# Splits and a product taken from GpSimd in the recurrent and gated-output stage of a hybrid S5 / RG-LRU block

## The chip, the cores and the metric

The kernel runs on one core of a Trainium2 chip. The metric is the device time of one execution in microseconds (us), the median over runs. Before the change it is 2388.78 us (three runs, 2385.07 to 2389.40).

In the text PE is the tensor engine, VectorE is DVE in the rows, ScalarE is ACT, GpSimd is POOL, and SP is the queue that issues the transfers.

## The reference

One layer of a diffusion backbone on 2048 latent tokens of 1024 channels, with 256 context tokens as prefix. What the change touches is the mixer's second half:

```
xc = centred_depthwise_conv(to_col_major(xr), conv_w, conv_b)          # 512 channels
for each direction d:
    r = sigmoid(block_diag(xc, w_rg[d], b_rg[d]));  i = sigmoid(block_diag(xc, w_ig[d], b_ig[d]))
    a = exp(-8 * r * softplus(-lam[d]))
    h[d] = linear_scan(a, sqrt(1 - a^2) * (i * xc))                    # along the sequence
y_lru = from_col_major(h[0] + h[1]) * gelu(gate)
y_s5  = y * sigmoid(y @ w_glu + b_glu)                                 # y: the S5 output, 512 channels
out   = concat(y_s5, y_lru) @ w_out
```

After it come a normed residual and a SwiGLU feed-forward network (FFN), which take the last 1460 us of the kernel.

## The kernel before

All matmuls are done in a split form: an fp32 operand is cut into a high part `hi`, a rounded copy in the matmul's type, and a low part `lo = src - hi`, and three matmuls (hi by hi, hi by lo, lo by hi) replace one. `split` writes `hi` on ScalarE (line 59) and `lo` on VectorE (line 62). `hi(..., nc.gpsimd)` (line 57) and `lo(..., nc.gpsimd)` put them on GpSimd.

The stage of interest runs from about 600 to 926 us. It has two parts that are woven into each other.

`lru` goes through four blocks m of 128 channels, each with 2308 positions (context, padding and latent). Per block: `conv(m)` loads the input, splits the gate weights (`lwh`, `lwl`), convolves on VectorE and splits the result in five chunks (`xh`, `xl`). `gates(m, d)`, for each direction, does twelve matmuls for each of the five chunks, evicts them with two sigmoids on ScalarE (`lr`, `li`, line 900) and multiplies `li` by `xc` (line 903). `decay` has Tanh, Exp and two Squares on ScalarE and two VectorE instructions per direction (lines 912 to 918). `scans` has a Sqrt on ScalarE, a product and two scans on VectorE (lines 922 to 929). Then both directions are added, multiplied by the gate branch, and stored to `YLRU`.

The filler is `glu` and `out_s5`. A `glu` step takes 256 tokens: load `gy`, split it (`gyh`, `gyl`), 48 matmuls, four VectorE bias adds from PSUM (line 1022), one Sigmoid on ScalarE (line 1023), one product, one store. There are eight. An `out_s5` tile takes 128 tokens: load `osy`, split it (`osyh`, `osyl`), and for each half of the 1024 output columns 12 matmuls and an eviction to `oso` (line 1048), then one store. There are sixteen tiles; each of `osy`, `osyh`, `osyl` and `oso` has two buffers.

How they are woven: `run` in `mix` steps `lru`, and each of its yields gives a credit of filler time, from which filler steps are traced:

```
for want in gen:
    owed += want
    while owed > 0:
        owed -= next(fill, 1e9)
```

Followed through, the credits place `glu` step 0 after `decay` of block 0, and steps 1 to 7 inside the gates of blocks 1 and 2. The splits of the `w_out` rows (`woh`) come near the end of the gates of block 2. `out_s5` tiles 0 to 2 lie inside the gates of block 3, and the first half of tile 3 after `decay` of block 3. The rest of the tiles are drained afterwards in `mix3`.

The order of the instructions on the engines is set by a planner that simulates a timeline, with one exception: `mix2` traces the loop under

```
with self.tc.manual_schedule(engines={self.nc.scalar.engine}):
    run(lru, fill)
```

so that ScalarE's instructions of this part stand in the order in which the program writes them. What is traced outside that block (the first `conv` in `mix`, the drain in `mix3`) is ordered by the planner on all engines. `glu` and `out_s5` are generators, so their steps are traced under whichever block pulls them.

After the stage, `tile_out` of the FFN reads `OSD` (the stored `out_s5` tiles) and `YLRU` and starts the second half of the output projection.

Of the kernel before, what the change touches and what calls it, by code (L numbers as in the profile page):

```python
# [12 lines left out]
AF = mybir.ActivationFunctionType  # L13
ALU = mybir.AluOpType
MUL, ADD, SUB = ALU.mult, ALU.add, ALU.subtract
# [30 lines left out]
class Hybrid:  # L46
# [783 lines left out]
    def lru(self, es, bes):  # L830


        nc, A, v = self.nc, self.A, self.nc.vector
# [26 lines left out]
        def conv(m):  # L860
            xs = p.tile([128, XC], F32, name="xs")
            nc.gpsimd.memset(xs[:, 0:2], 0.0)
            nc.gpsimd.memset(xs[:, 2 + CTX:2 + LAT], 0.0)
            nc.gpsimd.memset(xs[:, XC - 1:XC], 0.0)
            nc.sync.dma_start(xs[:, 2:2 + CTX], self.XRD[m][:, 0:CTX])
            nc.sync.dma_start(xs[:, 2 + LAT:XC - 1], self.XRD[m][:, CTX:CTX + SEQ])
            wr = p.tile([128, 4, 128], F32, name="lwr")
            wh, wl = (p.tile([128, 4, 128], F32R, name=nm, bufs=2) for nm in ("lwh", "lwl"))
            nc.gpsimd.memset(wr, 0.0)
            for i, nm in enumerate(("lru_w_rg", "lru_w_ig")):  # L870
                for h in range(2):
                    hs = slice(h * 64, (h + 1) * 64)
                    nc.sync.dma_start(wr[hs, i::2, hs], A[nm][0, :, 2 * m + h].rearrange("d a b -> a d b"))
            self.hi(wh, wr, nc.gpsimd)
            self.lo(wl, wr, wh, nc.gpsimd)
            xc = p2.tile([128, XO + 1], F32, name="xc")
            cw = lambda i: cB[:, C_CW + i * 4 + m:C_CW + i * 4 + m + 1]
            nc.gpsimd.memset(xc[:, XO:], 0.0)
            v.tensor_scalar(xc[:, :XO], xs[:, 0:XO], cw(0), cB[:, C_CB + m:C_CB + m + 1], op0=MUL, op1=ADD)
            for i in range(1, 4):  # L880
                v.scalar_tensor_tensor(xc[:, :XO], xs[:, i:i + XO], cw(i), xc[:, :XO], op0=MUL, op1=ADD)
            parts = []
            for j, (c0, n) in enumerate(CH):
                xh, xl = (p.tile([128, n], F32R, name=f"{nm}{j}") for nm in ("xh", "xl"))
                if m == 0:
                    self.split(xh, xl, xc[:, c0:c0 + n])
                else:
                    self.hi(xh, xc[:, c0:c0 + n], nc.gpsimd)
                    self.lo(xl, xc[:, c0:c0 + n], xh, nc.gpsimd)
                parts.append((xh, xl))  # L890
            return wh, wl, parts, xc

        def gates(m, d, wh, wl, parts, xc):
            ri = [(pb.tile([128, XO + 1], F32, name=nm, bufs=1) if (2 * m + d) % 3 == 2 else
                   p2.tile([128, XO + 1], F32, name=nm)) for nm in ("lr", "li")]
            for (c0, n), (xh, xl) in zip(CH, parts):
                for gt, cb in ((0, C_BRG), (1, C_BIG)):
                    pg = (psb if gt else ps).tile([128, 512], F32, name="pg")
                    self.mm3(pg[:, :n], wh[:, d * 2 + gt], wl[:, d * 2 + gt], xh, xl, True, True)
                    nc.scalar.activation(ri[gt][:, c0:c0 + n], pg[:, :n], AF.Sigmoid,  # L900
                                         bias=cB[:, cb + d * 4 + m:cb + d * 4 + m + 1])
                yield self.GATES_FILL[m]
            nc.gpsimd.tensor_tensor(ri[1], ri[1], xc, op=MUL)
            self.rit = ri

        H = (XO + 1) // 2
# [25 lines left out]
        self.wgraw = p2.tile([128, XO + 1], F32, name="xc")[:, :4 * 512].rearrange("p (k f) -> p k f", k=4)  # L932
        nc.sync.dma_start(self.wgraw, A["s5_w_glu"][0].rearrange("(k p) f -> p k f", p=128))
        x = conv(0)
        yield None
        pb = self.pool(bes, "lrub", 2, side="right")
        psb = self.pool(bes, "lrupsb", 2, side="right", space=PSUM)
        yield self.CONV_FILL
        ri = []
        for d in range(2):  # L940
            yield from gates(0, d, *x)
            ri.append(self.rit)
        for m in range(4):
            ts = [decay(m, d, ri[d][0]) for d in range(2)]
            if m == 3:

                raws = [p2.tile([128, XO + 1], F32, name="xc") for _ in range(2)]
                self.woraw = [self.raw_w_out(raws[k // 2][:, k % 2 * D:(k % 2 + 1) * D], 4 + k) for k in range(4)]
            else:
                x = conv(m + 1)  # L950
# [9 lines left out]
            if m < 3:  # L960
                yield from gates(m + 1, 0, *x)
                nxt.append(self.rit)
            gg = ri[1][1][:, :SEQ]
            nc.sync.dma_start(gg, self.GGD[m])
            y = ts[0]
# [4 lines left out]
            if m < 3:  # L970
                yield from gates(m + 1, 1, *x)
                nxt.append(self.rit)
            ri = nxt
# [20 lines left out]
    def glu(self, es):  # L994

        nc, A, v = self.nc, self.A, self.nc.vector
        p = self.pool(es, "gw", 1, side="right")
        st = self.pool(es, "gst", 2, side="right")
        ps = self.pool(es, "gps", 4, side="right", space=PSUM)
        wg = []  # L1000
        for k in range(4):
            wh, wl = p.tile([128, 512], F32R, name=f"wgh{k}"), p.tile([128, 512], F32R, name=f"wgl{k}")
            self.split(wh, wl, self.wgraw[:, k])
            wg.append((wh, wl))
        W = 256
        yield 0.1
        for n in range(8):
            y = st.tile([128, 4, W], F32, name="gy", bufs=3)
            nc.sync.dma_start(y, self.YD[:, :, n])
            yh, yl = st.tile([128, 4, W], F32R, name="gyh"), st.tile([128, 4, W], F32R, name="gyl")  # L1010
            self.hi(yh, y, nc.gpsimd)
            self.lo(yl, y, yh)
            z = st.tile([128, 4, W], F32, name="gz")
            for m in range(4):
                if m % 2 == 0:
                    pgs = ps.tile([128, 2, W], F32, name="pgl")
                pg = pgs[:, m % 2]
                ms = slice(m * 128, (m + 1) * 128)
                for k in range(4):
                    self.mm3(pg, wg[k][0][:, ms], wg[k][1][:, ms], yh[:, k], yl[:, k], k == 0, k == 3)  # L1020
                b = self.colsB[:, C_BGLU + m:C_BGLU + m + 1]
                v.tensor_scalar(z[:, m], pg, b, None, op0=ADD)
            nc.scalar.activation(z, z, AF.Sigmoid)
            v.tensor_tensor(z, z, y, op=MUL)
            nc.sync.dma_start(self.YS5[:, :, n * W:(n + 1) * W], z)
            yield 5.2

    def out_s5(self, es):

        nc, v = self.nc, self.nc.vector  # L1030
        wop = self.pool(es, "wo_a", 1, side="right")
        p = self.pool(es, "osp", 2, side="right")
        ps = self.pool(es, "osps", 4, side="right", space=PSUM)
        wo = self.split_w_out(wop, self.woraw)
        yield 10.0
        for i in range(16):
            y = p.tile([128, 4, 128], F32, name="osy")
            nc.sync.dma_start(y, self.YS5[:, :, i * 128:(i + 1) * 128])
            yh, yl = p.tile([128, 4, 128], F32R, name="osyh"), p.tile([128, 4, 128], F32R, name="osyl")
            self.hi(yh, y, nc.gpsimd)  # L1040
            self.lo(yl, y, yh)
            o = p.tile([128, D], F32, name="oso")
            for h in range(2):
                cs = slice(h * 512, (h + 1) * 512)
                po = ps.tile([128, 512], F32, name="pgl")
                for k in range(4):
                    self.mm3r(po, yh[:, k], yl[:, k], wo[k][0][:, cs], wo[k][1][:, cs], k == 0, k == 3)
                self.nc.vector.tensor_copy(o[:, cs], po)
                if h:
                    nc.sync.dma_start(self.OSD[i], o)  # L1050
                yield 2.6
# [475 lines left out]
```

## Time and profile before

| | us |
|---|---|
| median of three runs | 2388.78 |
| the profiled execution, its own time | 2388.56 |
| its span, first to last instruction | 2386.5 |
| PE busy in the span | 2125.2 |
| VectorE busy | 1750.7 |
| GpSimd busy | 1087.1 |
| ScalarE busy | 910.2 |

The profile is of one execution. Busy times do not add up to the span, since the engines work side by side. In the page's 40 slices PE shows nine tenths or more from slice 20 (1134 us) to slice 39. The stage of interest is slices 11 to 16, where PE shows 5, 4, 7, 7, 8, 8 tenths and VectorE 5, 8, 9, 8, 8, 6.

### The profile page before, as it was taken

What the parts mean: (1) busy time and instruction counts of PE and PEld (TensorE: products, weight loads), DVE (VectorE), ACT (ScalarE), POOL (GpSimd) and SP (SyncE); (2) the same over time, 40 slices, a digit from 0 to 9 for tenths busy, and PEclk for the clock granted to TensorE, in tenths of its full rate; (3) what the DMA queues carried; (4) which work ended last, traced back from release to release, by engine and by line L of the source; (5) the groups of instructions that cost most, each with busy time, mean ns of one, the idle gap of its engine ahead of it and who ended that gap; (6) DMA issues with size and microseconds to landing.
All of it is one profiled execution on the core that took longest, in us unless ns stands there. A gap on an engine that the chain in (4) does not pass through costs nothing. (4 is left out here: it accounts for less than half of the span.)

```text
span 2386.5 us, 27505 instructions
## 1 busy us (share of the span) xinstructions
PE 2125.2 (89%) x9460; PEld 1671.8 (70%) x9460; DVE 1750.7 (73%) x2293; ACT 910.2 (38%) x1434; POOL 1087.1 (46%) x665
## 2 busy tenths in 40 slices
PE   6689999896547788868999999999999999999997
PEld 2667776564436566756888888788888878888785
DVE  6975348969589886995777887987978763534688
ACT  3456521210266551554333333533333333232433
POOL 3655360325464532563333553665656530500584
PEclk8799999997678799978999999999999999999998
DMA  9465766654322447874344332554434464734583
GB/s 275 126 202 188 236 183 185 205 178 145 130 75 98 146 145 248 287 242 148 124 147 139 112 106 97 185 173 137 159 133 159 133 245 162 240 108 137 190 288 108
DMA packets 309387, 401.19 MB, mean 168 GB/s; under 512 B 59984, under 2 KB 220288, under 8 KB 307712
## 3 DMA queue, kind: packets, MB, share of 16 engines
q1 hardware_dynamic: 309120, 399.40, 51.5%
q8 instruction: 75, 1.23, 0.2%
q14 instruction: 64, 0.52, 0.1%
q0 software_dynamic: 128, 0.04, 0.0%
HBM read 268.28 MB, written 131.07 MB: 167 GB/s over the span
## 5 line engine op out<-in xcount | busy, mean ns | idle before, releaser
L70 PE MATMUL fp<-op,fws 128*128 128x512 f32 x1232 | 487.1, 396 | 9.9 <-DVE oy L1148 5.2
L71 PE MATMUL fp<-op,fws 128*128 128x512 f32 x1232 | 486.3, 395 | 4.0 <-DVE op L62 2.6
L72 PE MATMUL fp<-op,fws 128*128 128x512 f32 x1232 | 485.6, 394 | 0.0
L70 PEld LDWEIGHTS fp<-op,fws 128*128 128x128 f32 x1232 | 233.0, 189 | 64.9 <-ACT op L59 7.2
L71 PEld LDWEIGHTS fp<-op,fws 128*128 128x128 f32 x1232 | 233.3, 189 | 59.1 <-DVE op L62 4.4
L72 PEld LDWEIGHTS fp<-op,fws 128*128 128x128 f32 x1232 | 233.0, 189 | 52.1
L990 PE MATMUL po<-gw,ga 128*128 128x512 f32 x616 | 240.2, 391 | 5.2 <-ACT ga L59 2.7
L991 PE MATMUL po<-gw,ga 128*128 128x512 f32 x616 | 240.0, 391 | 0.1
L992 PE MATMUL po<-gw,ga 128*128 128x512 f32 x616 | 236.7, 390 | 2.7 <-DVE ga L62 2.7
L1284 POOL TENSOR_TENSOR fs<-fraw 128x512 f32<-128x512 f32 x44 | 64.9, 1475 | 338.3 <-DMA fraw<-in_w_ffn_in_dram 276.4
L70 PE MATMUL pu<-ht,winh 128*128 128x512 f32 (+1 forms) x448 | 176.4, 401 | 19.0 <-ACT ut L390 9.4
L71 PE MATMUL pu<-ht,winh 128*128 128x512 f32 (+1 forms) x448 | 174.7, 392 | 10.7 <-DVE ht L62 10.6
L72 PE MATMUL pu<-ht,winl 128*128 128x512 f32 (+1 forms) x448 | 172.5, 386 | 0.0
L62 DVE TENSOR_TENSOR fws<-fraw,fws 128x512 fp32r<-128x512 f32 x132 | 131.7, 999 | 48.1 <-ACT fws L59 47.2
L990 PEld LDWEIGHTS po<-gw,ga 128*128 128x128 f32 x616 | 116.2, 189 | 30.4 <-ACT ga L59 3.1
L59 ACT ACTIVATE fws<-fraw 128x512 fp32r<-128x512 f32 x132 | 82.7, 628 | 141.4 <-PE fp L72 74.5
L62 DVE TENSOR_TENSOR fws<-fs,fws 128x512 fp32r<-128x512 f32 x132 | 128.4, 973 | 9.4 <-ACT fws L59 7.3
L992 PEld LDWEIGHTS po<-gw,ga 128*128 128x128 f32 x616 | 115.5, 188 | 27.9 <-DVE ga L62 3.9
L991 PEld LDWEIGHTS po<-gw,ga 128*128 128x128 f32 x616 | 116.2, 189 | 24.8 <-DVE gw L62 0.5
L62 DVE TENSOR_TENSOR ga<-gys,ga 128x1024 fp32r<-128x1024 f32 (+2 forms) x88 | 116.5, 1328 | 12.1 <-ACT ga L59 12.0
L59 ACT ACTIVATE fws<-fs 128x512 fp32r<-128x512 f32 x132 | 82.4, 625 | 101.9 <-PE fp L72 99.0
L70 PEld LDWEIGHTS pu<-ht,winh 128*128 128x128 f32 x448 | 86.3, 195 | 45.3 <-ACT ut L390 10.3
(514 smaller groups left out, 4685.3 us busy)
## 6 DMA issues: line engine op xcount, KB each, us to landing
fraw<-in_w_ffn_in_dram SPq DMA_DIRECT2D x88, 512.0 KB, 4.4
graw<-in_w_ffn_out_dram SPq DMA_DIRECT2D x99, 256.0 KB, 3.4
gys<-S SPq DMA_DIRECT2D x44, 512.0 KB, 4.2
A<-faf SPq DMA_DIRECT2D x33, 512.0 KB, 2.6
S<-ost SPq DMA_DIRECT2D x33, 512.0 KB, 3.1
alw<-in_w_ada_dram SPq DMA_DIRECT2D x24, 512.0 KB, 4.0
ost<-A SPq DMA_DIRECT2D x22, 512.0 KB, 3.9
gys<-A SPq DMA_DIRECT2D x22, 512.0 KB, 4.8
```

Source lines behind the costliest of these rows:

```text
L59: self.nc.scalar.activation(hi, src, AF.Identity)
L62: (eng or self.nc.vector).tensor_tensor(lo, src, hi.bitcast(F32), op=SUB)
L70: mm(ps, wh, xh, start=first, stop=False)
L71: mm(ps, wh, xl, start=False, stop=False)
L72: mm(ps, wl, xh, start=False, stop=last)
L990: mm(ps, xh, wh, start=first, stop=False)
L991: mm(ps, xh, wl, start=False, stop=False)
L992: mm(ps, xl, wh, start=False, stop=last)
L1284: g.tensor_tensor(s[0], a21, a22, op=ADD)
```

## The change

Every operation that the stage gave to GpSimd, apart from memsets, is moved. The splits of the gate weights, of the convolved input of blocks 1 to 3, of the `glu` input and of the `out_s5` input become plain `split` calls: `hi` on ScalarE, `lo` on VectorE. The product of input gate and input (line 903) goes to VectorE. Of the two evictions of an `out_s5` tile the first goes to ScalarE, the second stays on VectorE. Tiles, buffers, transfers, credits and matmuls stay as they are.

```diff
-            self.hi(wh, wr, nc.gpsimd)
-            self.lo(wl, wr, wh, nc.gpsimd)
+            self.split(wh, wl, wr)
...
-                if m == 0:
-                    self.split(xh, xl, xc[:, c0:c0 + n])
-                else:
-                    self.hi(xh, xc[:, c0:c0 + n], nc.gpsimd)
-                    self.lo(xl, xc[:, c0:c0 + n], xh, nc.gpsimd)
+                self.split(xh, xl, xc[:, c0:c0 + n])
...
-            nc.gpsimd.tensor_tensor(ri[1], ri[1], xc, op=MUL)
+            v.tensor_tensor(ri[1], ri[1], xc, op=MUL)
...
-            self.hi(yh, y, nc.gpsimd)
-            self.lo(yl, y, yh)
+            self.split(yh, yl, y)          # glu, and the same in out_s5
...
-                self.nc.vector.tensor_copy(o[:, cs], po)
+                if h:
+                    v.tensor_copy(o[:, cs], po)
+                else:
+                    nc.scalar.activation(o[:, cs], po, AF.Copy)
```

## Rows read from the trace of the kernel before

**Rows 1.** Windows: engine busy us (instructions), PE's granted clock, DMA share, GB/s.
```profile
634.00:660.00 26.00, 26.00 (x164) 23.62 (x163) 19.57 (x22) 14.45 (x23) 14.97 (x14) 0.95 0.26 92
660.00:734.00 74.00, 38.98 (x224) 34.59 (x223) 62.33 (x35) 38.62 (x40) 48.33 (x30) 0.77 0.32 103
797.00:851.00 54.00, 45.53 (x190) 36.12 (x190) 48.24 (x30) 33.20 (x34) 21.09 (x11) 0.87 0.41 130
880.00:926.00 46.00, 36.75 (x156) 28.26 (x155) 34.62 (x32) 0.63 (x1) 11.08 (x9) 0.97 0.64 204
```

**Rows 2.** Waits of ScalarE, 630 to 880: total us, times, longest us.
```profile
ACT gz L1023 <- DVE gz L1022: 43.7, 4, 17.6
ACT lr L900 <- PE pg L72: 24.1, 15, 5.0
ACT lsq L917 <- DVE lt L918: 11.0, 7, 3.8
ACT lt L922 <- DVE lt L918: 5.9, 3, 2.5
```

**Rows 3.** Timeline of ScalarE: start us, us, instruction, idle before and releaser.
```profile
712.34 1.06 ACT L1023 ACTIVATE gz<-gz 128x1024 f32<-128x1024 f32 x1 [17.57 <-DVE gz L1022]
713.30 0.67 ACT L900 ACTIVATE lr<-pg,colsB 128x512 f32<-128x512 f32 x1
...
870.68 3.88 ACT L59 ACTIVATE woh<-xc 128x1024 fp32r<-128x1024 f32 x4
874.57 2.14 ACT L922 ACTIVATE lt<-lt 128x2308 f32<-128x2308 f32 x1
```

**Rows 4.** Groups of ScalarE, 600 to 925: busy us, mean ns, idle before.
```profile
L922 ACT ACTIVATE lt<-lt 128x2308 f32<-128x2308 f32 x8 | 17.1, 2134 | 5.9 <-DVE lt L918 5.9
L1023 ACT ACTIVATE gz<-gz 128x1024 f32<-128x1024 f32 x8 | 8.6, 1069 | 43.8 <-DVE gz L1022 43.7
L59 ACT ACTIVATE woh<-xc 128x1024 fp32r<-128x1024 f32 x4 | 3.9, 1042 | 0.0
L59 ACT ACTIVATE xh<-xc 128x512 fp32r<-128x512 f32 x4 | 2.2, 614 | 0.0
```

**Rows 5.** Groups of GpSimd, 600 to 925.
```profile
L903 POOL TENSOR_TENSOR li<-li,xc 128x2308 f32<-128x2308 f32 x8 | 51.4, 6427 | 14.6 <-ACT li L900 14.6
L57 POOL TENSOR_SCALAR gyh<-gy 128x1024 fp32r<-128x1024 f32 x8 | 15.4, 1929 | 6.0 <-PE pgl L72 3.5 <-DMA gy<-YD 2.5
```

**Rows 6.** Groups of VectorE, 600 to 925.
```profile
L908 DVE TENSOR_TENSOR_SCAN lt<-lr,lt,li 128x2048 f32<-128x2048 f32 x8 | 37.9, 4746 | 0.0
...
L62 DVE TENSOR_TENSOR osyl<-osy,osyh 128x512 fp32r<-128x512 f32 x16 | 24.3, 1520 | 1.3 <-POOL osyh L57 1.3
...
L923 DVE TENSOR_TENSOR li<-li,lt 128x2308 f32<-128x2308 f32 x8 | 20.5, 2574 | 0.0
L62 DVE TENSOR_TENSOR gyl<-gy,gyh 128x1024 fp32r<-128x1024 f32 x8 | 18.8, 2365 | 9.5 <-POOL gyh L57 9.5
...
L1022 DVE TENSOR_SCALAR gz<-pgl,colsB 128x256 f32<-128x256 f32 x32 | 14.2, 472 | 6.5 <-PE pgl L72 6.5
...
L62 DVE TENSOR_TENSOR xl<-xc,xh 128x512 fp32r<-128x512 f32 x4 | 2.5, 678 | 0.0
...
L62 DVE TENSOR_TENSOR wol<-lsq,woh 128x1024 fp32r<-128x1024 f32 x2 | 2.3, 1210 | 0.0
```

**Rows 7.** Timeline of PE: a glu product, the end of the out tiles, the FFN's start.
```profile
701.40 0.28 PE L72 MATMUL pgl<-gyh,wgl 128*128 128x256 f32 x1
...
703.80 0.28 PE L72 MATMUL pgl<-gyh,wgl 128*128 128x256 f32 x1
...
914.58 0.39 PE L990 MATMUL pgl<-woh,osyh 128*128 128x512 f32 x1
...
917.75 0.39 PE L992 MATMUL pgl<-woh,osyl 128*128 128x512 f32 x1
925.79 0.80 PE L990 MATMUL fpg<-woh,oyh 128*128 128x512 f32 x1 [7.65 <-ACT oyh L59]
```

More of the change, by code (lines that the diff above doesn't have):

```diff
@@ L1039, in out_s5 @@
             yh, yl = p.tile([128, 4, 128], F32R, name="osyh"), p.tile([128, 4, 128], F32R, name="osyl")
-            self.hi(yh, y, nc.gpsimd)
-            self.lo(yl, y, yh)
+            self.split(yh, yl, y)
             o = p.tile([128, D], F32, name="oso")
```

## The prediction, made before the changed kernel ran

> **What bounds the kernel now.** I read the page's slices first: the FFN keeps PE full, the stage that the change touches does not. Then the windows of that stage [rows 1]. In 660 to 734 us, the pass from block 0 to block 1, VectorE is busy 62 of 74 us, PE 39, ScalarE 39: no engine is full, so a chain through several engines sets the pace. The waits of ScalarE say which. It waits 43.7 us for the last bias add of a `glu` step, 24.1 us for gate matmuls, 11.0 and 5.9 us for VectorE's part of `decay` [rows 2]. The timeline shows that these waits are a matter of order: the Sigmoid of `glu` step 2 waits 17.6 us, and the gate sigmoid written behind it starts only then [rows 3]. ScalarE runs what `mix2` traces in program order, as the code asks. Only what is traced outside that block slips in, as the four `woh` splits of `mix3` between the last two Sqrts [rows 3]. The chain of this stage is therefore ScalarE's own list, from the gates of block 0 (634 to 660 [rows 1]) to the last Sqrt, which ends at 876.7 us [rows 3]. The out tiles run beside it on PE and end at 917.75 + 0.23 = 918 us. The FFN's first matmul follows at 925.8 [rows 7]. ScalarE has 0.6 us of work in the last 46 us [rows 1].
>
> **What it costs, by that list.** In every `glu` step the old `hi` ran on GpSimd, out of the list, so PE could multiply steps ahead while ScalarE was in gates or `decay`. Now `hi` of step n stands in the list, and the next entry of the list is the Sigmoid of the same step n: nothing is written between them. So from `hi` to Sigmoid ScalarE is held through a round of the other engines. Queued behind it are gate sigmoids; PE waits for their PSUM banks, and VectorE's scans wait for them too.
>
> (a) The `glu` steps. One round is: `hi` 1.04 (nearest row, a split of the same shape, [rows 4]), `lo` 1.21 (the same shape alone, [rows 6]), 48 matmuls, one bias add 0.47 [rows 6], Sigmoid 1.07 [rows 4]. The matmuls start 0.12 us apart (701.40 to 703.80 is 20 steps [rows 7]): 5.8 us. Sum 9.6. To this come the signals between engines and a VectorE that is busy: between 0 and one scan of 4.75 [rows 6]; I take 1.9, nearer to nothing, since VectorE is idle a sixth of the time. PE's granted clock is 0.77 on average in 660 to 734 [rows 1]; at the lower of its levels (1.2 instead of 2.4 GHz) the matmuls take 11.6, which I keep for the upper end. So 11.5 a step, 92 for eight. Before, eight Sigmoids and their waits cost 8 x 1.07 + 43.7 = 52.3 [rows 2, 4]. Term: +40; bounds 8 x 9.6 - 52 = +25 and 8 x (9.6 + 4.75 + 2) - 52 = +79, the 2 being a third of the slow matmuls' surplus.
>
> (b) The splits of `conv`. In blocks 1 to 3 six `hi` (one of weights, five of chunks) enter the list after `decay`, at most 0.61 each [rows 4]: 3 x 6 x 0.61 = +11. The convolution itself ran a block ahead on VectorE, so they need not wait. If that lead were gone, each block would wait for four passes of about 2.6 us (the nearest row, a product of the same length [rows 6]), 10 us, three times.
>
> (c) The out tiles. Tiles 0 to 3 have their `hi` in the list, and behind it the first eviction of the same tile, again with nothing between: `hi` 0.61, `lo` 0.68 [rows 6], 12 matmuls at 0.226 (914.58 to 917.75 is 14 steps [rows 7]) 2.7, a Copy of that shape 0.61 (nearest row, from SBUF), signals 0.4: 5.0. Four times: +20.
>
> (d) What falls. In 634 to 660 PE is full with the first gates and with three `glu` products that now come later [rows 1]; the 60 gate matmuls alone need 48 x 0.226 + 12 x 0.12 = 12.3, with a slow start and the last sigmoids about 17 of the 26 us: -9. The waits in `decay`, 11.0 and 5.9, fall on a VectorE slowed beside GpSimd: -17 at most, which I take. Of the 24.1 us for gate matmuls I take half, -12: in the gates of block 3 PE was multiplying out tiles, which (c) now contains. The first nine fell above.
>
> List: +40 + 11 + 20 - 38 = +33. The last Sqrt ends at about 910 instead of 876.7.
>
> (e) The end of the stage. Before, out tiles started near 802 and were done 918, in PE's gaps of the gates and `decay` of blocks 2 and 3: PE is busy 45.5 of the 54 us of 797 to 851 [rows 1]. Now tile 0 starts only in the gates of block 3, and the first half of tile 3 is done just ahead of the last two Sqrts (2 x 2.13 [rows 4], and about one more for what stands between): 910 - 5 = 905. Then 25 halves of 12 matmuls remain: 25 x 2.7 = 68, ending about 973, some 54 us later than 918. The later tiles' ScalarE work is not in the list, and `osy` has two buffers. Tile 4 can use the one that tile 3 does not hold, and go ahead during `decay` of block 3. I take two tiles, 11 us: the shift is +43. Not at all is the upper bound (+54), all through the gates of block 3 the lower: another 17 us, three tiles, +26.
>
> (f) What costs nothing. VectorE gets eight products of 2.57 [rows 6] and the `lo` of weights and chunks (at most 19 of 0.68, 13), 34 in all, and gives up 16 evictions of about 0.68, 11. It also loses its slow cases: `gyl` takes 2.37 us on average against 1.21 for that shape alone, `osyl` 1.52 against 0.68, together 8 x 1.16 + 16 x 0.84 = 23 [rows 6]. So its load stays as it was and it does not become the bound; without the 23 it would be full in 660 to 734. The drained tiles' ScalarE work lies beside an idle ScalarE [rows 1]. The stores and loads move with their steps: the store of the last `glu` step and tile 0's load have the whole of `decay` of block 2 before ScalarE comes to tile 0. SP's queue holds what it held.
>
> The FFN then starts as long after the last out tile as before (8 us), and its work is unchanged. Total: 2388.6 (the profiled execution, 0.2 under the median) + 43 = **2431 us**.
>
> The Trainium skill (SBUF — State Buffer, "Who interferes with whom") says that a VectorE instruction with two SBUF inputs and a GpSimd instruction that reads SBUF exclude each other, the later one being fully blocked. The trace agrees: `gyl` at 2.37 us against 1.21, and on the other side 6.43 us for the GpSimd product that VectorE does in 2.57 [rows 5, 6]. By that rule alone this change should win, and that is the first rival.
>
> **Rivals.**
> 1. Faster: GpSimd is the late partner now. The 43.7 us at the Sigmoids come from `gyh` (1.93 on average [rows 5]) and `gyl` that block each other in the `glu` steps; the product on GpSimd adds 3.9 us per direction. If the planner places `lo` at once and `glu`'s matmuls meet a free PE, a step could be short. For it: 23 us of VectorE stretch, 51 us of GpSimd product. Against: a round has 9.6 us even with no wait. It decides at the point where a step from `hi` to the end of Sigmoid takes under 52.3 / 8 = 6.5 us plus what (d) gives, less (b): 6.5 + (38 - 11) / 8 = 9.9. Just below that the list breaks even; if the out tiles also run ahead as before, the time is 2388.6 less about half of the 23: 2377.
> 2. The list is longer but the out tiles swallow it: tiles from 4 on run through the gates of block 3, and rounds are short (9.6): 43 - 17 - 15 = +11, 2400.
> 3. VectorE becomes the bound of the rounds: each `lo` stands behind a scan, at 4.75 instead of the 1.9 taken, 8 x 2.85 = 23 more, and no tile goes ahead, 11 more: 43 + 23 + 11 = +77, 2466. Against it: VectorE's sixth of idle time [rows 1].
> 4. The order is kept only by the planner's choice, and it now puts `hi` ahead of the gates, so that the change does nothing but exchange engines: within 5 us, 2389.
>
> **How the numbers follow.** Chances: forecast 0.68, rival 1 0.10, rival 2 0.11, rival 3 0.08, rival 4 0.03. The range for 8 in 10 takes the forecast with its bounds, rival 2 for the most part, and not rivals 1 and 3: 2396 to 2460. A difference of under 0.2% (5 us) is not told from none here. Faster: rival 1 and a little of 4, 0.11. Same: the rest of 4, 0.02, and a sliver of rival 2, 0.01. Slower: 0.86.
>
> **What would show it.** In the trace after: on ScalarE each `gyh` is followed directly by its Sigmoid with an idle of 8 us or more before it, put down to the bias add; the sum of these waits is about 75 us instead of 43.7. The second `decay` starts later than 734 although the first starts some 9 us before 660. PE has a hole of 20 us or more between the last `glu` product and the first out tile. The last Sqrt ends near 910, the last out matmul near 960, and from the FFN's first matmul on all is shifted by that. `gyl` and `osyl` stand at 1.2 and 0.68 us. It is wrong if ScalarE does other work between `gyh` and its Sigmoid, if the waits for the bias add do not grow, or if the last out matmul stays near 918.

## The result, and the profile after

The changed kernel takes 2442.48 us (median of four runs, 2440.78 to 2449.13); the kernel before took 2387.84 beside it. The ratio is 1.0231, 95% interval 1.0209 to 1.0253: slower by 54.6 us. The forecast was 2431 in a range of 2396 to 2460. The profiled execution took 2440.78 us with a span of 2439.0.

The windows of the stage, in the columns of [rows 1]:

```profile
634.00:660.00 26.00, 8.35 (x33) 6.09 (x32) 22.59 (x13) 25.68 (x28) 0.79 (x5) 0.66 0.13 46
660.00:734.00 74.00, 45.77 (x250) 40.39 (x251) 48.95 (x42) 25.54 (x32) 0.26 (x4) 0.80 0.31 103
797.00:851.00 54.00, 25.77 (x131) 21.91 (x130) 30.31 (x29) 38.21 (x41) 0.00 (x0) 0.69 0.18 61
880.00:926.00 46.00, 30.45 (x128) 24.22 (x127) 30.73 (x23) 31.69 (x31) 0.00 (x0) 0.85 0.29 97
```

Between 660 and 734 us ScalarE, which was given more work, is busy 25.5 us instead of 38.6, and VectorE 49 instead of 62 [rows 1]. In 797 to 851, where PE did out tiles before, PE is busy 25.8 of 54 us instead of 45.5. GpSimd has next to nothing left (0.8 us at most). These windows stand still while the work in them has moved, so the whole stage is the fairer measure: from 600 us to the FFN's first matmul (926 us before, 981 after) VectorE is busy 245.0 us instead of 262.8, PE 229.5 instead of 215.1 and ScalarE 188.5 instead of 155.4, in 55 us more. All three have more idle time than before, VectorE most. That points to waiting, though ScalarE has 33 us more work too; the experiments tell the two apart.

The waits of ScalarE say where. These are the totals of 600 to 960 us, as in [rows 2]:

```profile
ACT gz L1017 <- DVE gz L1016: 93.8, 8, 16.5
ACT oso L1044 <- PE pgl L987: 24.9, 6, 12.1
...
ACT lr L895 <- PE pg L72: 1.2, 2, 0.9
```

The wait at the Sigmoid of the `glu` steps has gone from 43.7 us in four steps to 93.8 in all eight. A wait at the evictions of the out tiles is new. The waits for gate matmuls (24.1 us) are nearly gone, those in `decay` (11.0 and 5.9) wholly. A further 20.9 us, for stores of `oso`, lie in the drained tiles behind the written list.

The timeline of ScalarE shows the form of it, for a `glu` step, the first out tile, and the last two Sqrts:

```profile
682.24 1.07 ACT L59 ACTIVATE gyh<-gy 128x1024 fp32r<-128x1024 f32 x1
698.81 1.06 ACT L1017 ACTIVATE gz<-gz 128x1024 f32<-128x1024 f32 x1 [15.50 <-DVE gz L1016]
699.77 0.67 ACT L895 ACTIVATE lr<-pg,colsB 128x512 f32<-128x512 f32 x1
...
854.10 0.62 ACT L59 ACTIVATE osyh<-osy 128x512 fp32r<-128x512 f32 x1
866.79 0.60 ACT L1044 ACTIVATE oso<-pgl 128x512 f32<-128x512 f32 x1 [12.07 <-PE pgl L987]
...
908.65 4.16 ACT L917 ACTIVATE lt<-lt 128x2308 f32<-128x2308 f32 x2
```

The split and its own Sigmoid are neighbours, and ScalarE stands still between them. Six gate sigmoids are done in one run right behind (the row of 699.77 is the first of them). Four of them had been ready since 686.2 us, when the last of their matmuls ended; PE did those of the other two only when the first sigmoids had run. The last Sqrt ends at 912.8 us; before it was 876.7 [rows 3].

How the stage ends, on PE (to be read beside [rows 7]):

```profile
980.67 0.39 PE L987 MATMUL pgl<-woh,osyl 128*128 128x512 f32 x1
980.89 0.39 PE L985 MATMUL fpg<-woh,oyh 128*128 128x512 f32 x1
```

The last out matmul starts 63 us later than before (917.75), but the FFN's first matmul stands directly behind it, without the 8 us gap. It is 55.1 us late (925.79), and that is the whole loss: the span grew by 52.5.

VectorE's groups show what the change does give, in the columns of [rows 6]:

```profile
L898 DVE TENSOR_TENSOR li<-li,xc 128x2308 f32<-128x2308 f32 x8 | 20.4, 2555 | 6.1 <-ACT li L895 6.1
...
L62 DVE TENSOR_TENSOR osyl<-osy,osyh 128x512 fp32r<-128x512 f32 x16 | 11.6, 723 | 4.3 <-ACT osyh L59 4.3
...
L62 DVE TENSOR_TENSOR gyl<-gy,gyh 128x1024 fp32r<-128x1024 f32 x8 | 9.8, 1220 | 3.8 <-ACT gyh L59 3.8
```

The product takes 2.56 us instead of 6.43 on GpSimd [rows 5], and the low parts are at 1.22 and 0.72 instead of 2.37 and 1.52.

### The profile page after: what moved, and what is told of

Read it like the earlier page. It is cut to its first block, busy times and chain, and to the rows that moved or that the text cites. A ratio compares the mean times of both kernels' runs of the same rounds, so it can differ in the third digit from the quotient of the medians.

```text
span 2439.0 us, 27527 instructions
## 1 busy us (share of the span) xinstructions
PE 2139.1 (88%) x9460; PEld 1682.0 (69%) x9460; DVE 1754.6 (72%) x2304; ACT 944.0 (39%) x1493; POOL 938.2 (38%) x595
## 5 line engine op out<-in xcount | busy, mean ns | idle before, releaser
L62 DVE TENSOR_TENSOR fws<-fraw,fws 128x512 fp32r<-128x512 f32 x132 | 140.4, 1065 | 44.7 <-ACT fws L59 43.9
```

Of the source, the lines that this page charges most:

```text
L62: (eng or self.nc.vector).tensor_tensor(lo, src, hi.bitcast(F32), op=SUB)
```

## The experiments

Theory *order*: in ScalarE's written list each split now stands right ahead of the Sigmoid or eviction that needs it, so ScalarE is held through a round of VectorE and PE, and the list behind it too. Rival *load*: the moved operations cost their own time on engines that had none to spare. Ratios are to the kernel before, with 95% intervals; its median beside E1 to E4 was 2390.2, beside E5 to E8 2389.3, beside E9 to E12 2389.6.

**E1: the `glu` split back on GpSimd, the rest as changed.**

```diff
-            self.split(yh, yl, y)          # glu
+            self.hi(yh, y, nc.gpsimd)
+            self.lo(yl, y, yh)
```

> The changed kernel with one edit undone: the high part of the eight glu steps goes back to GpSimd, and so leaves ScalarE's written list. Theory order (ScalarE is held from each gyh to the Sigmoid of the same step): the wait for the bias add falls from 93.8 us to about 40 (43.7 in the kernel before), the list gets some 55 to 60 us shorter, the out tiles begin that much earlier, and the time is about 2390 us. Theory load (the moved work itself costs, not where it stands): only 8 x 1.05 us leave ScalarE, so about 2434 us. Rival, the out tiles are the bound and not the glu steps: the last out matmul stays near 980 us and the time stays within 10 us of 2442.

2398.71 us, ratio 1.0033 (1.0018 to 1.0048): 44 us of the loss are gone for 8.6 us of work taken from ScalarE. Its wait at the Sigmoid is

```profile
ACT gz L1018 <- DVE gz L1017: 32.5, 4, 12.3
```

Load is out by a factor of five for this part.

**E2: the out tiles as before, the rest as changed** (split on GpSimd, both evictions on VectorE).

```diff
-            self.split(yh, yl, y)          # out_s5
+            self.hi(yh, y, nc.gpsimd)
+            self.lo(yl, y, yh)
...
+                self.nc.vector.tensor_copy(o[:, cs], po)   # both halves
```

> The changed kernel with the out tiles as before: high part on GpSimd, both evictions on VectorE. The glu steps stay held. Theory order: the waits of ScalarE for out matmuls (24.9 us) and the four splits leave the list, the first out tile follows the woh splits (about 823 us) instead of 854, and the last out matmul comes at about 930 instead of 981; the time is about 2400 us. Theory load: 16 splits of 0.63 and 16 evictions of 0.60 leave ScalarE, about 20 us that lay partly beside an idle ScalarE, and VectorE gets 11 us back: 2430 to 2445 us. Rival, the glu steps alone make the loss: the time stays within 10 us of 2442.

2409.59 us, ratio 1.0084 (1.0061 to 1.0107): 33 us are gone, while the `glu` waits stay at 93.7. The out tiles now end at 935 us, nearer to the expected 930 than to 981. The rival "`glu` alone" falls.

**E3: same engines, same work, the `glu` split written one step ahead.**

```diff
+        nxt = ahead(0)                     # load and split of step 0
         for n in range(8):
+            y, yh, yl = nxt
...
             nc.sync.dma_start(self.YS5[:, :, n * W:(n + 1) * W], z)
+            if n < 7:
+                nxt = ahead(n + 1)
```

> The changed kernel with the same work on the same engines; load and split of glu step n+1 are written right behind the store of step n, so that gates stand between gyh and its Sigmoid. Theory order: the waits at the bias add fall from 93.8 to 30 to 45 us, and the time falls by 45 to 60 us, to about 2390. Theory load: no work is taken away, so the time stays at 2442 within 8 us. This is also the version that might stand beside the kernel before without GpSimd.

2419.37 us, ratio 1.0123 (1.0096 to 1.0149): 23 us faster than the changed kernel with nothing taken away, which load can't explain, but half of what order expected. The waits that are left:

```profile
ACT gz L1023 <- DVE gz L1022: 61.2, 6, 14.1
```

Two of eight steps no longer wait. In five of the others four to six gate sigmoids between split and Sigmoid (2 to 3 us) are too little cover for a round of ten and more. The longest wait, 14.1 us, has 8 us of cover by Sqrts and sigmoids; there the last two bias adds stand behind two scans on VectorE (8.84 us from 680.04).

**E4: the kernel before with the product alone on VectorE.**

```diff
-            nc.gpsimd.tensor_tensor(ri[1], ri[1], xc, op=MUL)
+            v.tensor_tensor(ri[1], ri[1], xc, op=MUL)
```

> The kernel before with one edit of the change: the product of input gate and input goes from GpSimd (6.43 us each, eight times) to VectorE (2.57 each). Nothing enters ScalarE's list. Theory order: this part of the change is harmless or a gain, since gyl, osyl and the decay products are no longer slowed beside it: 2375 to 2388 us. Theory load on VectorE (it is the busiest engine of the stage, 62 of 74 us): 20 us more on it show, about 2400 us.

2365.4 us, ratio 0.9901 (0.9871 to 0.9930): faster by 25 us, more than expected. This one line of the change is a gain. VectorE's other groups are quicker for it, though GpSimd still does the splits that it did before. Compare [rows 6], and the last row here, which is of the kernel before:

```profile
L903 DVE TENSOR_TENSOR li<-li,xc 128x2308 f32<-128x2308 f32 x8 | 22.3, 2787 | 2.0 <-ACT li L900 2.0
...
L62 DVE TENSOR_TENSOR gyl<-gy,gyh 128x1024 fp32r<-128x1024 f32 x8 | 11.9, 1502 | 10.0 <-POOL gyh L57 9.0 <-POOL xc L878 0.9
L62 DVE TENSOR_TENSOR osyl<-osy,osyh 128x512 fp32r<-128x512 f32 x16 | 11.3, 706 | 0.7 <-POOL osyh L57 0.7
L1024 DVE TENSOR_TENSOR gz<-gz,gy 128x1024 f32<-128x1024 f32 x8 | 11.1, 1382 | 1.1 <-ACT gz L1023 1.1
...
L1024 DVE TENSOR_TENSOR gz<-gz,gy 128x1024 f32<-128x1024 f32 x8 | 18.6, 2329 | 2.2 <-ACT gz L1023 2.2
```

`gyl` and `osyl` give back 6.9 + 13.0 = 20 us of VectorE and the product of the `glu` steps (`gz`) another 7.5, which is more than the 22.3 that the moved product adds; and that product itself is 3.6 us shorter per direction.

**E5: the changed kernel without the written order.**

```diff
-        with self.tc.manual_schedule(engines={self.nc.scalar.engine}):
-            run(lru, fill)
+        run(lru, fill)
```

> The changed kernel without the written order of ScalarE in this part: the planner orders all engines, the work is the same. Theory order: no split has to stand right ahead of its own Sigmoid or eviction; the waits at the bias add (93.8 us) and at the out matmuls (24.9) fall by more than half and the time lies between 2385 and 2415 us. Theory load: the engines do the same work, so the time stays at 2442 within 10 us. Rival: the written order was worth more than the hold costs (the planner's own order delays decay and Sqrt), and the time is over 2450.

2374.05 us, ratio 0.9939 (0.9921 to 0.9957): 68 us less than the changed kernel, and faster than the kernel before, with every operation on the engine that the change gave it. The planner puts other work between split and Sigmoid, and VectorE is then busy 72.8 of the 74 us between 660 and 734; the wait for the bias add is

```profile
ACT gz L1016 <- DVE gz L1015: 4.7, 1, 4.7
```

**E9: the control, the kernel before without the written order** (the same two lines).

> The kernel before without the written order of ScalarE, as the control of the run of the changed kernel without it (2374). Theory order: in the kernel before the splits were out of the list, so the list costs it little; 2375 to 2395 us, a gain of less than a third of the 68 us that the changed kernel had. Rival, the written order is a loss for any version and says nothing of the change: the kernel before gains as much, 2325 to 2350 us.

2388.01 us, ratio 0.9989 (0.9972 to 1.0006): no difference. The written order cost the kernel before nothing and costs the changed kernel 68 us. E5 and E9 together settle the main point: the loss needs the pair of order and split, neither makes it alone.

**E6: `glu` and out tiles as before; of the change only the product and the splits of `conv` and of the gate weights stay.**

> The changed kernel with glu step splits and out tiles as before; what stays of the change is the product on VectorE and the splits of the gate weights and of the convolved input. Theory order: the two undone parts were found to cost 44 and 33 us; if these add, the time is about 2365 us, near the 2365 of the product alone. Since three times 3.1 us of splits stay in the list, 2365 to 2375. Rival, the two losses overlap (one delay hides the other): 2385 to 2400. Theory load on VectorE: the splits of the chunks (13 us) show as well, 2380 or more.

2364.43 us, ratio 0.9897 (0.9882 to 0.9913). The two losses add: 44 + 33 = 77, and 2442.5 - 2364.4 = 78. Beside E4 the 18 splits in the list, with what they relieve on GpSimd, cost nothing that shows.

**E7: the kernel before with the `glu` split alone on ScalarE. E8: with the out tiles alone.**

> The kernel before with one edit: the high part of the glu steps on ScalarE. Theory order: the waits at the bias add rise from 43.7 to 90 us or more, the list gets about 30 us longer after the first gates have given some back, and the time is about 2418 us. Theory load: 8 x 1.05 us on an engine that is busy 38 of 74 us: 2388 to 2396 us.

> The kernel before with the out tiles of the change alone: high part on ScalarE, first eviction on ScalarE. Theory order: tiles 0 to 3 enter the list, four rounds of about 6 us; the first tile starts some 30 us after the woh splits instead of 6, the last out matmul comes 25 to 35 us later; part of that is taken back because the next stage no longer waits 8 us at its start: 2408 to 2418 us. Theory load: VectorE is relieved of 11 us and of its slow cases beside GpSimd, 2380 to 2388 us.

E7: 2428.31 us, ratio 1.0167 (1.0144 to 1.0190), 39 us slower. E8: 2413.93 us, ratio 1.0102 (1.0082 to 1.0122), 25 us slower. Load expected a gain in E8. In E7 the wait is longer than in the changed kernel, probably since GpSimd's product still slows VectorE inside the round (`gyl` takes 2.29 us there on average, 1.22 in the changed kernel):

```profile
ACT gz L1022 <- DVE gz L1021: 104.3, 8, 19.9
```

From the kernel before, the parts sum to 39 + 25 - 25 = +39, and the whole is +54.6. So 15 us come of their meeting. The runs show where: product and `conv` splits together gain 25 us where neither other part is in (E6), 19 beside the held `glu` steps (E7 to E2) and 15 beside the out tiles (E8 to E1). Whether the product gains less where ScalarE is held anyway, or the `conv` splits cost something there, was not separated.

**E10: E6 without the written order.**

> The version of 2364 us (product and convolution splits as in the change, glu splits and out tiles as before) without the written order: is there more to be had? If the waits that are left (31 us at the bias add, 25 at gate matmuls) come from the order, 2340 to 2355 us; if they come from the work of PE and VectorE itself, 2360 to 2375.

2362.33 us, ratio 0.9878 (0.9850 to 0.9905): the fastest of all, but not told from E6 (their intervals overlap). The planner's free order finds nothing more in this version. E5 differs from E10 by the `glu` splits and the out tiles alone, and is 11.7 us slower: of the 78 us that these two parts cost, some 12 stay with a free order and 66 go with the written one. So load, or what the planner makes of it, has a share too, of some 15%.

**E11 and E12: why a round takes longer than forecast.** Both start from the changed kernel. E11 gives each column group a PSUM bank of its own; E12 takes the bias add from VectorE into four Sigmoids on ScalarE.

```diff
-                if m % 2 == 0:
-                    pgs = ps.tile([128, 2, W], F32, name="pgl")
-                pg = pgs[:, m % 2]
+                pg = ps.tile([128, 512], F32, name="pgl")[:, :W]      # E11
...
-                v.tensor_scalar(z[:, m], pg, b, None, op0=ADD)
-            nc.scalar.activation(z, z, AF.Sigmoid)
+                nc.scalar.activation(z[:, m], pg, AF.Sigmoid, bias=b) # E12
```

> The changed kernel, but each of the four column groups of a glu step gets a PSUM bank of its own instead of two in one, so that PE need not wait for VectorE's bias add between two groups of a bank. Same work, same order. If the extra length of a round (13.9 us instead of the 11.5 of the prediction) comes from this second trip, the waits at the bias add fall from 93.8 to 75 to 82 us and the time falls by 10 to 18, to about 2428. If it comes from the last bias add alone, or from lo, standing behind scans, waits and time stay: 2436 to 2446 us.

> The changed kernel, with the bias add of the glu steps taken into ScalarE's Sigmoid: four Sigmoids of 256 columns straight from PSUM replace four adds on VectorE and one Sigmoid. ScalarE has some 1 us more per step, VectorE leaves the second half of the round. If VectorE's queue makes the rounds long, a round falls from 13.9 to 10 to 11 us and the time by 20 to 30, to about 2415; if PE's matmuls and clock make it, the time stays within 8 us of 2442.

E11: 2444.02 us, ratio 1.0219 (1.0187 to 1.0251): no effect on the time; the wait is

```profile
ACT gz L1015 <- DVE gz L1014: 91.7, 8, 13.8
```

E12: 2430.1 us, ratio 1.0164 (1.0136 to 1.0192): 12 us faster than the changed kernel. That is between the two expectations: the bias adds' place in VectorE's queue is a part of the long rounds. ScalarE still waits 73.7 us, now for PE. But PE in turn still waits for VectorE, since the low part stays in its queue. In the longest round of E12, 18.4 us, `gyh` starts at 698.49, and these are the low part and the matmul that needs it:

```profile
706.26 1.22 DVE L62 TENSOR_TENSOR gyl<-gy,gyh 128x1024 fp32r<-128x1024 f32 x1
...
707.53 0.58 PE L71 MATMUL pgl<-gyl,wgh 128*128 128x256 f32 x1 [6.88 <-DVE gyl L62]
```

So E12 does not tell what the whole of VectorE's queue is worth.

## Why the prediction came out as it did

The mechanism was the one forecast, and each sign of it was in the trace: splits and Sigmoids as neighbours, the wait at the bias add up, the hole on PE ahead of the out tiles, the last Sqrt late, the FFN shifted as a whole. Of its signs, the hold is 7.6 us at least, near the forecast 8. The hole on PE is 20.2 us and ends with the `xh` split of block 3, which stands in the list as well:

```profile
841.23 2.07 PE L70 MATMUL pg<-xh,lwh 128*128 128x512 f32 x4 [20.19 <-ACT xh L59]
```

By step:

(a) The rounds were mis-sized. A step from `gyh` to the end of its Sigmoid takes 93.8 (waits) + 8 x 1.07 + 8 x 1.06 and one table load of 1.3, 112 us in all, 14.0 each; the forecast was 11.5. So the term is +60 (112 - 52.3), not +40. The floor was right: the shortest round is 9.8 us (716.82 to 726.59), forecast 9.6. The longest is 18.6 (771.61 to 790.24). What makes the difference shows in the round of 682 us, on VectorE and PE:

```profile
683.35 1.23 DVE L62 TENSOR_TENSOR gyl<-gy,gyh 128x1024 fp32r<-128x1024 f32 x1 [0.47 <-ACT gyh L59]
684.49 8.86 DVE L903 TENSOR_TENSOR_SCAN lt<-lr,lt,li 128x2048 f32<-128x2048 f32 x2
693.26 0.85 DVE L1016 TENSOR_SCALAR gz<-pgl,colsB 128x256 f32<-128x256 f32 x2
```

```profile
693.77 0.58 PE L70 MATMUL pgl<-gyh,wgh 128*128 128x256 f32 x1 [4.49 <-DVE gz L1016]
```

The bias adds stand behind two scans of 4.4 us, and PE waits for them in turn. I had allowed 1.9 us per round for a busy VectorE, by its mean idle share. But the scans become ready just after the Sqrts, and that is where steps 1 and 5, the two longest rounds (17.6 and 18.6 us), begin. E12 puts the bias adds at 12 us. E11 shows that the shared banks are not it, though PE's wait in the rows above is real: without it ScalarE waits 13.8 us in steps 1 and 5 instead of 15.5 and 16.5, but longer in steps 2 and 6. Late low parts are in the trace too: in steps 0, 2, 4 and 6 `gyl` starts 6.6, 3.2, 2.7 and 2.7 us after its split begins, in the other four 1.1. How the remainder divides between these, gate matmuls queued ahead on PE and its granted clock (0.66 to 0.85 on average in the windows above) was not separated.

(b) The splits of `conv` take 3.0 us per block in the list, 9 in all, close to +11; E6 beside E4 shows them as nothing in the time. What the prediction did not count is that PE waits for them, 56.0 us in four places (the row of 841.23 is the longest); with the two other parts undone, in E6, it is 16.2.

(c) Tiles 0 to 2 take 13.3, 5.9 and 4.8 us from split to the end of the eviction, against the forecast 5.0: the low part of the first stood behind two scans again (`osyl` at 861.4). With tile 3, some 26 against +20.

(d) What falls was under-sized: the waits in `decay` went entirely, as taken, those for gate matmuls almost entirely (25 of 27), and the first gates ended 19 us earlier instead of 9: the first `decay` starts at 640.1 us. Of the 19, 7.4 lie before the gates. The `xh` splits of block 0 begin at 624.2 us instead of 631.6, because a sum on GpSimd that ScalarE and PE wait for (`alacc`) is done that much earlier; the prediction had no term for it.

So the list grew by 36 us (912.8 against 876.7), forecast +33: too little in (a) and too little given back in (d) met. In sums, 60 + 9 + 26 = 95 us were added and 59 given back, where the forecast gave back 38. Of the 59, 17 are the waits in `decay`, 25 those for gate matmuls, 7.4 the earlier start and 4.5 a wait for a scan; 5 were not traced.

(e) Two more errors that partly cancel. No tile went ahead of tile 3 during the last `decay`; tile 4's split comes at 905.3 us, after it. The 11 us taken for that were wrong. The 25 halves behind tile 3's first also took 74 us instead of 68 (906.7 to 981), and PE ends at 981 instead of 961. Against that, the gap before the FFN did not stay: while the out tiles still ran, its loads had landed and its first split was done at 953 us, so 8 us came back. 63 - 8 = 55 is the measured shift.

That the total came within 12 us is in part luck. Rival 3 asked for 23 us more in the rounds and 11 more because no tile goes ahead; the rounds were 20 longer and no tile went ahead, so both came nearly in full, though more by bias adds behind scans than by each `lo`. They did not make its 2466 because (d) gave back 21 us more than forecast and the gap before the FFN another 8.

(f) The product was costed at nothing beside the relief of VectorE, and the relief counted in (d) only through `decay`. E4 puts it at -25 us. Here is the largest thing the prediction did not see: on top of that gain the two held parts cost about 78 us (E6 to the changed kernel). The rule of the Trainium skill that the prediction weighed (SBUF — State Buffer, "Who interferes with whom"), that a VectorE instruction with two SBUF inputs and a GpSimd instruction that reads SBUF exclude each other, agrees with E4: `osyl` and `gyl` became shorter when GpSimd lost its largest instruction. The prediction's other figure for it, 6.43 us on GpSimd against 2.57, is weaker: the shortest of the eight still takes 5.08 there (the mean is in [rows 5]). What the rule could not tell is the price of the splits' new place.

The first rival was right in its reason and wrong in its sum: the relief is real, but it comes from one line, and the two held parts cost three times as much.

The Trainium skill (Perfetto Trace Analysis, "Identifying the Most-Contended Engine") tells to look for the engine with the highest occupancy and improve that one. Here the stage's busiest engine was VectorE with 62 of 74 us; the change took 18 us of work off it over the whole stage (262.8 to 245.0) and the kernel lost 54.6 us, while E4, which added the product to it, gained 25. The trace does not bear the advice out for a stage that is paced by a chain: what counted was who waits between two neighbours of one engine's list.

## What to carry to other kernels

Where an engine's order is written out, an operation moved onto it takes a place in that order. Before moving it, look at its next neighbour in the list: if that one needs the result by way of other engines, the engine is held for the whole round, here 14 us on average for a split of 1.07. A helper engine that looks slow can be worth keeping for being outside the list; and a change made of several moves is best timed move by move, since here one line alone was 25 us faster and two others cost 77.

## What the runs showed of the hardware

Taking one two-input product of 128x2308 off GpSimd made VectorE's own instructions shorter: the same `osyl` went from 1.52 to 0.71 us on average and `gyl` from 2.37 to 1.50, with GpSimd's splits still running (E4). In the changed kernel, with GpSimd all but empty, they are 0.72 and 1.22. It is not free for all that stays on GpSimd: between the kernel before and E4 its `xh` splits went from 1.26 us to 1.91 and `lwl` from 1.53 to 2.67, while `gyh` fell from 1.93 to 1.59. That VectorE's eight added products lengthen the two is likely, but was not shown. GpSimd's groups in the columns of [rows 5], first of the kernel before, then of E4:

```profile
L57 POOL TENSOR_SCALAR xh<-xc 128x512 fp32r<-128x512 f32 x12 | 15.0, 1258 | 28.0 <-PE pg L72 28.0
...
L62 POOL TENSOR_TENSOR lwl<-lwr,lwh 128x512 fp32r<-128x512 f32 x4 | 6.1, 1526 | 0.1
...
L57 POOL TENSOR_SCALAR xh<-xc 128x512 fp32r<-128x512 f32 x12 | 22.9, 1907 | 32.6 <-PE pg L72 32.6
...
L62 POOL TENSOR_TENSOR lwl<-lwr,lwh 128x512 fp32r<-128x512 f32 x4 | 10.7, 2672 | 0.1
```

An eviction of 128x512 from PSUM takes 0.60 us on ScalarE (the 12 us before it are a wait) and 0.69 on VectorE in the changed kernel, so it was not the eviction's own duration that cost.
